# Eight wide products and then eight narrow ones, with the weight buffers 64 bytes apart, in a one-core hybrid trunk layer

## The chip, the cores and the metric

The kernel runs on one NeuronCore of a Trainium2 chip. The metric is the device time of one execution in microseconds (us). Engines are named as the profile names them: PE is TensorE's matmul, PEld its weight load, DVE is VectorE, ACT ScalarE, POOL GpSimd, SP SyncE, whose queue issues most DMAs.

## What is computed

One layer over 256 tokens of width 2048 in float32: a norm, a wide input projection whose columns feed four head groups, an output projection, a second norm and a SwiGLU.

```python
def reference(x, norm_mix_g, w_in, ..., w_out, norm_ffn_g, w_gate, w_up, w_down):
    h = x
    for l in range(DEPTH):                       # DEPTH = 1
        u = rmsnorm(h, norm_mix_g[l])
        h = h + hybrid_mixer(u, w_in[l], ..., w_out[l])   # conv, pooling, linear attention, attention
        u = rmsnorm(h, norm_ffn_g[l])
        h = h + swiglu_ffn(u, w_gate[l], w_up[l], w_down[l])
    return h

def swiglu_ffn(u, w_gate, w_up, w_down):
    return (jax.nn.silu(u @ w_gate) * (u @ w_up)) @ w_down
```

D_MODEL is 2048, D_FF 5632. The four groups are a gated convolution (A), multi-scale pooling (B), gated linear attention (C: its output is normed per head and gated) and forgetting attention (D).

## The kernel before

**Precision.** Every float32 value x that enters a large product is split into a rounded part hi (float32r, written by a cast on ACT) and the rest lo = x - hi (DVE). A product of weights and activations is then three products: weights hi with activations hi, weights hi with activations lo, weights lo with activations hi. Activations sit in SBUF as `u`, `y` and `hT`, shaped [128, k, 2, 256]: for each block k of 128 features first the 256 tokens' hi, then their lo. So hi weights are multiplied with 512 columns at once (hi and lo side by side, a *wide* product) and lo weights with 256 (a *narrow* product, added to the lo half of the same PSUM bank). `halves` adds the two halves of a bank at the end.

**Chunks.** All weights lie in one array `wall` of 376 chunks of 128 x 1024 in the order of use. `stage_through` issues for each the DMA into `raw` (4 buffers), the cast into `hi` on ACT (line 114) and the subtraction into `lo` on DVE (line 115), LOOK = 3 chunks ahead of use. `hi` and `lo` have four buffers each.

**Stages.** `block_lead` takes chunks 0 to 7, `block_tm` the next 40 (tokens on the partitions; its three products per k are all 512 columns wide, lines 203 to 205), then `block_fm` everything else: 8 blocks of the input projection (steps 2 or 4), 8 of the output projection with `y`, 44 of gate and up with `u`, and 8 of the down projection with `hT`. The last of these 8 is the `tail` (lines 169 to 171, all products 256 wide). A block of `block_fm` has 16 k (4 chunks) or 44 k (11 chunks), and for each k two column halves m, each into its own bank.

**The pair.** In `block_fm`, for each k and m a narrow product (`rest`, line 155) and a wide one (`whole`, line 152) follow each other; only at a block's first k the wide one goes first. There are 317 chunks of this kind with 8 pairs each: 2536 pairs.

```python
for f in (whole, rest) if first else (rest, whole):
    f()
```

**The work beside it.** Everything else of the mixer is written as generators in the queue `tasks` (`others` for pooling and convolution). After each chunk `side(n)` advances the first generator by n `yield`s, so a `yield` moves what follows it later in the stream of products. A recording layer then orders each engine's instructions by priority. Three pieces matter here:
- `gla_out` (group C): after the head norms (`rsqrt_of`, lines 226 to 237) it waits 4 yields, multiplies `sgg` and `ob` (lines 490 and 492), and after 5 more yields PE transposes `ob` (line 502).
- `token_rstd` (lines 239 to 254), run for both norms: PE sums squares (line 244), DVE and ACT form the reciprocal root, DVE writes two diagonal matrices `dg` (line 251), PE multiplies each with ones (line 252).
- `rsqrt_of` refines the root by one Newton step on DVE (four operations after the reciprocal).

**Addresses.** In the built program `u`, `y`, `hT` and all eight `hi` and `lo` buffers begin at byte 128 modulo 512 of a partition. The slice that a product reads as weights (128 columns, 512 bytes) or as moving columns begins a multiple of 512 bytes further on. So the two streams that PE reads beside each other begin at the same place modulo 512 in all of these products.

Of the kernel before, what the change touches and what calls it, by code (L numbers as in the profile page):

```python
# [9 lines left out]
F32 = mybir.dt.float32  # L10
BF16 = mybir.dt.bfloat16
F32R = mybir.dt.float32r
U8 = mybir.dt.uint8
AF = mybir.ActivationFunctionType
ALU = mybir.AluOpType
AX = mybir.AxisListType

P = 128
T = 256
# [39 lines left out]
def trunk_kernel(ctx: ExitStack, tc: tile.TileContext, a, out):  # L59
    nc = tc.nc  # L60
    V, S, PE = nc.vector, nc.scalar, nc.tensor
# [3 lines left out]
    ev = ctx.enter_context(tc.tile_pool(name="ev", bufs=2))  # L65
# [38 lines left out]
    def stage_through(n, ahead=AHEAD, parts=1):  # L104
        while issued[0] <= min(n, total - 1):
            i = issued[0]
            raw = wpool.tile([P, 1024], F32, name="raw", bufs=4)
            hi = wpool.tile([P, 1024], F32R, name="hi")
            lo = wpool.tile([P, 1024], F32R, name="lo")
            with tc.high_priority(offset=ahead):  # L110
                for q in range(parts):
                    c = slice(q * 1024 // parts, (q + 1) * 1024 // parts)
                    nc.sync.dma_start(out=raw[:, c], in_=a["wall"][i][:, c])
                    S.copy(out=hi[:, c], in_=raw[:, c])  # L114
                    V.tensor_tensor(out=lo[:, c], in0=raw[:, c], in1=hi[:, c].bitcast(F32), op=ALU.subtract)  # L115
            staged[i] = (hi, lo)
            issued[0] += 1
# [18 lines left out]
    def block_fm(rhs, order, steps=0, tail=False):  # L136
        b = [acc(), acc()]
        n = len(order)
        for c0 in range(0, n, 4):
            hi, lo = next_chunk()  # L140
            hi = hi.rearrange("p (k c) -> p k c", k=4)
            lo = lo.rearrange("p (k c) -> p k c", k=4)
            for kk in range(4):
                k = order[c0 + kk]
                first, last = c0 + kk == 0, c0 + kk == n - 1
                if tail:
                    continue
                for m in range(2):
                    cs = slice(m * P, (m + 1) * P)

                    def whole():
                        PE.matmul(b[m], lhsT=hi[:, kk, cs], rhs=rhs[:, k], start=first, stop=last)  # L152

                    def rest():
                        PE.matmul(b[m][:, T:], lhsT=lo[:, kk, cs], rhs=rhs[:, k, 0], start=False, stop=False,  # L155
                                  skip_group_check=True)

                    for f in (whole, rest) if first else (rest, whole):
                        f()
            if tail:  # L160

                turns = [(kk, m) for kk in range(4) for m in range(2)]
                if c0 + 4 == n:
                    turns = [(kk, m) for m in range(2) for kk in range(4)]
                for kk, m in turns:
                    k = order[c0 + kk]
                    cs = slice(m * P, (m + 1) * P)
                    o = b[m][:, :T]
                    PE.matmul(o, lhsT=hi[:, kk, cs], rhs=rhs[:, k, 0], start=c0 + kk == 0, stop=False)  # L169
                    PE.matmul(o, lhsT=hi[:, kk, cs], rhs=rhs[:, k, 1], start=False, stop=False)  # L170
                    PE.matmul(o, lhsT=lo[:, kk, cs], rhs=rhs[:, k, 0], start=False, stop=c0 + kk == n - 1)  # L171
            side(steps)
            side(1, others)
        return b
# [52 lines left out]
    def rsqrt_of(dst, src, pool, mul, n):  # L227

        w = pool.tile([P, 64 if pool is ev else 3 * n], F32, name=f"rs{n}")
        v, r, q = [w[:, i * n:(i + 1) * n] for i in range(3)]  # L230
        V.tensor_scalar(out=v, in0=src, scalar1=mul, scalar2=EPS, op0=ALU.mult, op1=ALU.add)
        S.activation(out=r, in_=v, func=AF.Sqrt)
        V.reciprocal(out=r, in_=r)
        V.tensor_tensor(out=q, in0=r, in1=r, op=ALU.mult)
        V.tensor_tensor(out=q, in0=q, in1=v, op=ALU.mult)
        V.tensor_scalar(out=q, in0=q, scalar1=-0.5, scalar2=1.5, op0=ALU.mult, op1=ALU.add)
        V.tensor_tensor(out=dst, in0=r, in1=q, op=ALU.mult)

    def token_rstd(sq):


        ps = misc()
        for t in range(2):
            PE.matmul(ps[:, t:t + 1], lhsT=sq[:, t * P:(t + 1) * P], rhs=con[:, C_ONE:C_ONE + 1], start=True, stop=True)
        rsqrt_of(rcol, ps[:, 0:2], ev, 1.0 / D, 2)
        yield
        yield
        ps2 = misc()
        for t in range(2):
            dg = ev.tile([P, P], F32, name="dg")  # L250
            V.tensor_scalar(out=dg, in0=ident, scalar1=rcol[:, t:t + 1], scalar2=None, op0=ALU.mult)
            PE.matmul(ps2[:, t * P:(t + 1) * P], lhsT=ones, rhs=dg, start=True, stop=True)
        S.copy(out=rb, in_=ps2[:, :T])
        yield
# [214 lines left out]
    def gla_out(gv, sgg):  # L469
# [14 lines left out]
            yield  # L484
        rs = mx.tile([P, 8], F32, name="grs")
        rsqrt_of(rs, ss, mx, 1.0 / P, 8)
        for _ in range(4):
            yield
        obv = ob.rearrange("p t h v -> p (t h) v")
        V.tensor_tensor(out=sgg, in0=sgg, in1=obv, op=ALU.mult)  # L490
# [339 lines left out]
```

## Time and profile before

| | |
|---|---|
| median of 3 runs | 1105.49 us (1104.51 to 1106.24) |
| the profiled execution | 1106.24 us, of which the span from first to last instruction is 1104.4 us |
| PE busy | 1096.7 us, 99% of the span |
| PEld, DVE, ACT busy | 86%, 65%, 48% |
| granted TensorE clock | 0.998 of full speed on the mean |
| DMA | 203.81 MB, 185 GB/s on the mean |

Matmuls overlap in the array and their recorded ends are modelled: a wide product is shown as 398 ns, though the next one starts some 230 ns later. So a busy PE says little, and what one product costs is read from the distance between the starts of two that follow each other. The 1.84 us between the time and the span lie before the first and behind the last instruction.

### The profile page before, as it was taken

The page shows a single profiled execution, that of the slowest core. Times are in us where ns is not written, and L with a number is a line of the kernel's source. Part 1 is how long each engine was busy: PE and PEld are TensorE (multiplying, and loading weights), DVE is VectorE, ACT ScalarE, POOL GpSimd, SP SyncE. Part 2 cuts the span into 40 slices and gives each one's busy share as a digit, 9 for nine tenths or more (in the row PEclk, how much of TensorE's full clock was granted, in tenths as well). Part 3 has the DMA queues.
Part 4 walks back from the last instruction along what each step waited for, and adds up shares of the span by engine and source line. Part 5 has one row for each costly group of instructions (what it writes and reads, how often), then busy time and mean ns, then how long its engine had stood idle before and what let it go on. Part 6 is the DMA issues. An engine that isn't in the chain of part 4 may idle for free.

```text
span 1104.4 us, 16172 instructions
## 1 busy us (share of the span) xinstructions
PE 1096.7 (99%) x6300; PEld 950.9 (86%) x6300; DVE 721.7 (65%) x1000; ACT 528.4 (48%) x726; POOL 36.3 (3%) x35
## 2 busy tenths in 40 slices
PE   9999999999999999999999999999999999999998
PEld 8887788888888888888888888888888888888898
DVE  8798867886777766666666666666666444555442
ACT  8545544454545544454445444454445343334441
POOL 0000000000443100000000000000000000000000
PEclk9999999999999999999999999999999999999999
DMA  8655355455565556655665565556556666666661
GB/s 310 213 177 161 126 172 172 159 166 175 187 191 188 176 190 191 186 184 185 189 191 183 185 187 189 190 181 185 188 191 185 184 195 200 199 200 198 199 190 62
DMA packets 59725, 203.81 MB, mean 185 GB/s; under 512 B 6768, under 2 KB 9216, under 8 KB 59648
## 3 DMA queue, kind: packets, MB, share of 16 engines
q1 hardware_dynamic: 59504, 202.75, 58.6%
q8 instruction: 49, 0.80, 0.3%
q14 instruction: 28, 0.23, 0.1%
q10 hardware_dynamic: 144, 0.03, 0.0%
HBM read 200.65 MB, written 2.10 MB: 184 GB/s over the span
## 4 chain that ended last, share of the span: by engine, by line
PE 97%; DVE 1%; DMA 1%; ACT 1%; issue 0%; SPq 0%; DVEq 0%; ACTq 0%
PE acc L152 54%; PE acc L155 27%; PE acc L203 3%; PE acc L204 3%; PE acc L205 3%; PE acc L186 1%; PE acc L171 1%; PE acc L169 1%; PE acc L170 1%; PE misc L401 1%; DMA raw<-in_wall 1%; DVE lo L115 0%; PE acc L662 0%; ACT hi L114 0%; PE misc L565 0%
## 5 line engine op out<-in xcount | busy, mean ns | idle before, releaser
L115 DVE TENSOR_TENSOR lo<-raw,hi 128x1024 fp32r<-128x1024 f32 (+1 forms) x384 | 463.6, 1209 | 311.6 <-ACT hi L114 303.6
L114 ACT CAST hi<-raw 128x1024 fp32r<-128x1024 f32 (+1 forms) x384 | 395.7, 1031 | 433.1 <-PE acc L152 254.5
L152 PE MATMUL acc<-u,hi 128*128 128x512 f32 x1664 | 583.6, 398 | 0.0
L155 PE MATMUL acc<-u,lo 128*128 128x256 f32 x1664 | 460.9, 282 | 0.0
L152 PEld LDWEIGHTS acc<-u,hi 128*128 128x128 f32 x1664 | 310.0, 188 | 70.4
L155 PEld LDWEIGHTS acc<-u,lo 128*128 128x128 f32 x1664 | 314.4, 189 | 4.8
L152 PE MATMUL acc<-hT,hi 128*128 128x512 f32 x616 | 215.5, 397 | 0.0
L155 PE MATMUL acc<-hT,lo 128*128 128x256 f32 x616 | 171.1, 280 | 0.0
L152 PEld LDWEIGHTS acc<-hT,hi 128*128 128x128 f32 x616 | 115.4, 188 | 27.2
L155 PEld LDWEIGHTS acc<-hT,lo 128*128 128x128 f32 x616 | 116.1, 189 | 0.6
L212 ACT COPY t<-acc 128x256 f32<-128x256 f32 x134 | 48.8, 364 | 96.1 <-PE acc L152 96.1
L152 PE MATMUL acc<-y,hi 128*128 128x512 f32 x256 | 89.9, 398 | 0.0
L214 DVE TENSOR_TENSOR t<-acc,t 128x256 f32<-128x256 f32 x134 | 56.3, 420 | 38.5 <-ACT t L212 38.5
L155 PE MATMUL acc<-y,lo 128*128 128x256 f32 x256 | 70.7, 281 | 0.0
L203 PE MATMUL acc<-hi,u 128*128 128x512 f32 x160 | 64.5, 403 | 0.0
L204 PE MATMUL acc<-hi,u 128*128 128x512 f32 x160 | 63.3, 395 | 0.0
L205 PE MATMUL acc<-lo,u 128*128 128x512 f32 x160 | 63.2, 395 | 0.0
L152 PEld LDWEIGHTS acc<-y,hi 128*128 128x128 f32 x256 | 47.7, 188 | 11.1
L155 PEld LDWEIGHTS acc<-y,lo 128*128 128x128 f32 x256 | 48.4, 189 | 0.7
L203 PEld LDWEIGHTS acc<-hi,u 128*128 128x128 f32 x160 | 30.3, 190 | 7.0
L205 PEld LDWEIGHTS acc<-lo,u 128*128 128x128 f32 x160 | 30.5, 191 | 6.5
L204 PEld LDWEIGHTS acc<-hi,u 128*128 128x128 f32 x160 | 30.4, 190 | 6.2 <-issue 0.3
(198 smaller groups left out, 625.9 us busy)
## 6 DMA issues: line engine op xcount, KB each, us to landing
raw<-in_wall SPq DMA_DIRECT2D x368, 512.0 KB, 3.5
raw<-in_wall SPq DMA_DIRECT2D x16, 256.0 KB, 5.4
out_T<-t SPq DMA_DIRECT2D x16, 128.0 KB, 2.6
xT<-in_xT SPq DMA_DIRECT2D x7, 256.0 KB, 5.4
con<-in_con SPq DMA_DIRECT2D x1, 480.0 KB, 5.7
msk_raw<-in_msk SPq DMA_DIRECT2D x1, 448.0 KB, 6.1
xT<-in_xT SPq DMA_DIRECT2D x2, 128.0 KB, 2.7
poolw<-in_poolw SPq DMA_DIRECT2D x1, 256.0 KB, 4.7
```

Of the source, the lines that this page charges most:

```text
L114: S.copy(out=hi[:, c], in_=raw[:, c])
L115: V.tensor_tensor(out=lo[:, c], in0=raw[:, c], in1=hi[:, c].bitcast(F32), op=ALU.subtract)
L152: PE.matmul(b[m], lhsT=hi[:, kk, cs], rhs=rhs[:, k], start=first, stop=last)
L155: PE.matmul(b[m][:, T:], lhsT=lo[:, kk, cs], rhs=rhs[:, k, 0], start=False, stop=False, skip_group_check=True)
L169: PE.matmul(o, lhsT=hi[:, kk, cs], rhs=rhs[:, k, 0], start=c0 + kk == 0, stop=False)
L170: PE.matmul(o, lhsT=hi[:, kk, cs], rhs=rhs[:, k, 1], start=False, stop=False)
L171: PE.matmul(o, lhsT=lo[:, kk, cs], rhs=rhs[:, k, 0], start=False, stop=c0 + kk == n - 1)
L203: PE.matmul(b[t], lhsT=u[:, k, 0, ts], rhs=hi[:, kk], start=k == 0, stop=False)
L204: PE.matmul(b[t], lhsT=u[:, k, 1, ts], rhs=hi[:, kk], start=False, stop=False)
L205: PE.matmul(b[t], lhsT=u[:, k, 0, ts], rhs=lo[:, kk], start=False, stop=k == KT - 1)
L212: S.copy(out=t1, in_=bank[:, T:])
L214: V.tensor_tensor(out=t2, in0=bank[:, :T], in1=t1, op=ALU.add)
```

## The change

Five edits, the first two the larger ones:
1. In `block_fm` (outside the tail) a chunk's 8 wide products are issued in a row, then its 8 narrow ones. In a block's last chunk the narrow ones go first, so that the wide ones can close the sum.
2. The eight weight buffers become eight tiles of their own, each 1040 elements long of which 1024 are used: each begins 4160 = 8 x 512 + 64 bytes behind the one before. In the built program `hi0, lo0, hi1, lo1, hi2, lo2, hi3, lo3` begin at 128, 192, 256, 320, 384, 448, 0 and 64 modulo 512. `u`, `y` and `hT` stay at 128.
3. The Newton step takes two DVE operations in place of three behind the square.
4. `dg` has one buffer in place of two (the space for edit 2), so the second waits until PE has read the first.
5. `gla_out` waits 8 yields in place of 4.

```diff
-            hi = wpool.tile([P, 1024], F32R, name="hi")
-            lo = wpool.tile([P, 1024], F32R, name="lo")
+            hi, lo = [wpool.tile([P, 1040], F32R, name=f"{v}{i % 4}", bufs=1)[:, :1024] for v in ("hi", "lo")]
...
-                    for f in (whole, rest) if first else (rest, whole):
-                        f()
+            if not tail:
+                turns = [(kk, m) for kk in range(4) for m in range(2)]
+
+                def whole():
+                    for kk, m in turns:
+                        PE.matmul(b[m], lhsT=hi[:, kk, m * P:(m + 1) * P], rhs=rhs[:, order[c0 + kk]],
+                                  start=c0 + kk == 0, stop=c0 + kk == n - 1)
+
+                def rest():
+                    for kk, m in turns:
+                        PE.matmul(b[m][:, T:], lhsT=lo[:, kk, m * P:(m + 1) * P], rhs=rhs[:, order[c0 + kk], 0],
+                                  start=False, stop=False, skip_group_check=True)
+
+                for f in (rest, whole) if c0 + 4 == n else (whole, rest):
+                    f()
...
-        V.tensor_tensor(out=q, in0=q, in1=v, op=ALU.mult)
-        V.tensor_scalar(out=q, in0=q, scalar1=-0.5, scalar2=1.5, op0=ALU.mult, op1=ALU.add)
-        V.tensor_tensor(out=dst, in0=r, in1=q, op=ALU.mult)
+        V.scalar_tensor_tensor(out=q, in0=q, scalar=-0.5, in1=v, op0=ALU.mult, op1=ALU.mult)
+        V.scalar_tensor_tensor(out=dst, in0=q, scalar=1.5, in1=r, op0=ALU.add, op1=ALU.mult)
...
-            dg = ev.tile([P, P], F32, name="dg")
+            dg = ev.tile([P, P], F32, name="dg", bufs=1)
...
-        for _ in range(4):
+        for _ in range(8):
             yield
```

PE's order at the second norm, near the start of gate and up, before: behind the sums of squares (line 244) eleven pairs of a narrow and a wide product follow, of which the last stand here, then both products with `dg`.

```order
L155 MATMUL acc<-u,lo 128x256
L152 MATMUL acc<-u,hi 128x512
L155 MATMUL acc<-u,lo 128x256
L152 MATMUL acc<-u,hi 128x512
L252 MATMUL misc<-dg,con 128x128 x2
L155 MATMUL acc<-u,lo 128x256
L152 MATMUL acc<-u,hi 128x512
```

The same place in the change (line numbers are one or two lower; `hi_3518` and so on are the buffers' uses):

```order
L243 MATMUL misc<-con,sq 128x1 x2
L150 MATMUL acc<-u,hi_3518 128x512 x8
L155 MATMUL acc<-u,lo_3519 128x256 x8
L150 MATMUL acc<-u,hi_3540 128x512
L251 MATMUL misc<-dg,con 128x128
L150 MATMUL acc<-u,hi_3540 128x512 x6
L251 MATMUL misc<-dg,con 128x128
L150 MATMUL acc<-u,hi_3540 128x512
L155 MATMUL acc<-u,lo_3541 128x256 x8
L155 MATMUL acc<-u,lo_3565 128x256 x8
L150 MATMUL acc<-u,hi_3564 128x512 x8
```

Wide and narrow products now come in runs of eight, two runs of narrow ones join where a block's last chunk begins, and the first product with `dg` stands behind 9 wide and 8 narrow products in place of 11 and 11, the second six wide ones later.

DVE's order at the same norm, before:

```order
L234 TENSOR_TENSOR rs_3591<-rs_3591 128x2
L235 TENSOR_TENSOR rs_3591<-rs_3591 128x2
L236 TENSOR_SCALAR rs_3591<-rs_3591 128x2
L237 TENSOR_TENSOR rcol<-rs_3591 128x2
L251 TENSOR_SCALAR dg<-con,rcol 128x128 x2
L115 TENSOR_TENSOR lo<-raw,hi 128x1024
```

And in the change:

```order
L234 TENSOR_TENSOR rs_3588<-rs_3588 128x2
L235 SCALAR_TENSOR_TENSOR rs_3588<-rs_3588 128x2
L236 SCALAR_TENSOR_TENSOR rcol<-rs_3588 128x2
L250 TENSOR_SCALAR dg<-con,rcol 128x128
L115 TENSOR_TENSOR lo_3641<-raw,hi_3640 128x1024
L250 TENSOR_SCALAR dg<-con,rcol 128x128
```

One short operation is gone, and the subtraction of a chunk stands between the two `dg`.

PE's order where `gla_out` transposes, in the stage of `block_tm`, with the buffers' numbers, before: the four transposes stand between the chunks `hi_1249` and `hi_1276` of the block that fills `acc_1136` and `acc_1137`.

```order
L203 MATMUL acc_1137<-hi_1249,u_71 128x512
L204 MATMUL acc_1137<-hi_1249,u_71 128x512
L205 MATMUL acc_1137<-lo_1250,u_71 128x512
L502 MATMUL misc_1331<-con_73,ob_1224 128x128 x2
L502 MATMUL misc_1336<-con_73,ob_1224 128x128 x2
L203 MATMUL acc_1136<-hi_1276,u_71 128x512
L204 MATMUL acc_1136<-hi_1276,u_71 128x512
```

In the change, where the block's last chunk is `hi3_1274`:

```order
L203 MATMUL acc_1136<-hi3_1274,u_71 128x512
L204 MATMUL acc_1136<-hi3_1274,u_71 128x512
L205 MATMUL acc_1136<-lo3_1275,u_71 128x512
L501 MATMUL misc_1347<-con_73,ob_1223 128x128 x2
L203 MATMUL acc_1355<-hi0_1292,u_71 128x512
L204 MATMUL acc_1355<-hi0_1292,u_71 128x512
```

The first transposes stand one chunk, 12 wide products, later: 58 such products lie between them and the products of line 481 in place of 46. On DVE the row of line 492 that they wait for now comes one short operation and one cast (line 384, which moved behind it) earlier.

## Rows read from the trace of the kernel before

**Rows 1.** The page: busy us, share of the span, instructions; granted clock by slices.
```profile
PE 1096.7 (99%) x6300; PEld 950.9 (86%) x6300; DVE 721.7 (65%) x1000; ACT 528.4 (48%) x726; POOL 36.3 (3%) x35
...
PEclk9999999999999999999999999999999999999999
```

**Rows 2.** The page: the chain that ended last, shares of the span by line.
```profile
PE acc L152 54%; PE acc L155 27%; PE acc L203 3%; PE acc L204 3%; PE acc L205 3%; PE acc L186 1%; PE acc L171 1%; PE acc L169 1%; PE acc L170 1%; PE misc L401 1%; DMA raw<-in_wall 1%; DVE lo L115 0%; PE acc L662 0%; ACT hi L114 0%; PE misc L565 0%
```

**Rows 3.** Timeline of PE, gate and up: start us, us, what; ten pairs.
```profile
499.62 0.40 PE L152 MATMUL acc<-u,hi 128*128 128x512 f32 x1
499.85 0.28 PE L155 MATMUL acc<-u,lo 128*128 128x256 f32 x1
499.97 0.40 PE L152 MATMUL acc<-u,hi 128*128 128x512 f32 x1
500.21 0.28 PE L155 MATMUL acc<-u,lo 128*128 128x256 f32 x1
...
503.15 0.40 PE L152 MATMUL acc<-u,hi 128*128 128x512 f32 x1
```

**Rows 4.** Timeline of PE in `block_tm`: first and 25th of a row of wide products.
```profile
127.30 0.39 PE L203 MATMUL acc<-hi,u 128*128 128x512 f32 x1
...
132.74 0.39 PE L203 MATMUL acc<-hi,u 128*128 128x512 f32 x1
```

**Rows 5.** Timeline of PE in the tail: first and 25th of a row of narrow products.
```profile
1080.28 0.28 PE L169 MATMUL acc<-hT,hi 128*128 128x256 f32 x1
...
1083.15 0.28 PE L169 MATMUL acc<-hT,hi 128*128 128x256 f32 x1
```

**Rows 6.** Line 152 by operand: ns min/median/max, first and last start us.
```profile
L152 PE MATMUL acc<-hT,hi x616: 387/395/404, 853.6 to 1069.2; 128*128 128x512 f32 x154
...
L152 PE MATMUL acc<-y,hi x256: 386/398/404, 266.2 to 356.2; 128*128 128x512 f32 x128
```

**Rows 7.** Timeline of PE in the down projection: first and 13th wide product of pairs.
```profile
1009.75 0.39 PE L152 MATMUL acc<-hT,hi 128*128 128x512 f32 x1
...
1013.91 0.39 PE L152 MATMUL acc<-hT,hi 128*128 128x512 f32 x1
```

**Rows 8.** Timeline of PE at a block's end: two wide products, then the next narrow one.
```profile
503.51 0.62 PE L152 MATMUL acc<-u,hi 128*128 128x512 f32 x2
...
503.97 0.28 PE L155 MATMUL acc<-u,lo 128*128 128x256 f32 x1
```

**Rows 9.** Timeline of PE at the transposes of `ob`; idle time and its releaser in brackets.
```profile
135.23 0.39 PE L205 MATMUL acc<-lo,u 128*128 128x512 f32 x1
137.58 0.63 PE L502 MATMUL misc<-con,ob 128*128 128x128 f32 x4 [1.96 <-DVE ob L492]
...
139.48 0.63 PE L205 MATMUL acc<-lo,u 128*128 128x512 f32 x1
...
142.04 0.51 PE L205 MATMUL acc<-lo,u 128*128 128x512 f32 x1
```

**Rows 10.** The stretch behind it: busy us of PE, PEld, DVE, ACT, POOL; granted clock; DMA.
```profile
138.90:142.20 3.30, 3.30 (x10) 2.52 (x9) 2.13 (x4) 0.69 (x1) 0.00 (x0) 0.50 0.59 174
```

**Rows 11.** Timeline of DVE ahead of those transposes.
```profile
135.90 0.28 DVE L384 CAST fhl<-fe 4x256 fp32r<-4x256 f32 x1
136.21 1.23 DVE L492 TENSOR_TENSOR ob<-sgg,grs 128x1024 f32<-128x1024 f32 x1
```

**Rows 12.** Timeline of DVE at the second norm.
```profile
374.13 0.16 DVE L237 TENSOR_TENSOR rcol<-rs 128x2 f32<-128x2 f32 x1
374.33 0.48 DVE L251 TENSOR_SCALAR dg<-con,rcol 128x128 f32<-128x128 f32 x2
```

**Rows 13.** Timeline of PE there: the first product behind the sums, and those with `dg`.
```profile
370.91 0.37 PE L155 MATMUL acc<-u,lo 128*128 128x256 f32 x1
...
374.81 0.61 PE L252 MATMUL misc<-dg,con 128*128 128x128 f32 x4
```

**Rows 14.** Who PE waited for: us in total, times, longest.
```profile
PE acc L186 <- ACT hi L114: 0.9, 2, 0.5
```

More of the change, by code (lines that the diff above doesn't have):

```diff
@@ L142, in block_fm @@
             lo = lo.rearrange("p (k c) -> p k c", k=4)
[L143 to L156, printed above, removed]
-                    for f in (whole, rest) if first else (rest, whole):
-                        f()
+            if not tail:
[10 more added lines that the diff above has]
+                    f()
             if tail:
```

## The prediction

> **What bounds the kernel now.** The page says it at once: PE is busy for 99% of the span, at the full granted clock in every slice [rows 1], and the chain that ended last lies for 54% in the wide products of line 152 and for 27% in the narrow ones of line 155 [rows 2]. A busy PE does not show what a product costs, so I read next the timeline of PE and take the distance from start to start. In gate and up ten pairs of a wide and a narrow product take 503.15 - 499.62 = 3.53 us, 353 ns a pair: some 235 for the wide one, 118 for the narrow one [rows 3]. Two other stages show what products of one width cost when they follow each other. In `block_tm` 24 wide ones take 132.74 - 127.30 = 5.44 us, 226.7 ns each [rows 4]; in the tail 24 narrow ones take 2.87 us, 119.6 ns each [rows 5]. Together 346.3, so 6.7 ns less than the pair in alternation. That difference, 2536 times, is what edit 1 is about.
>
> The alternation isn't always so slow: late in the down projection 12 pairs take 4.16 us, 346.7 ns each [rows 7]. The stage means say where that happens. Gate and up last from behind the last product with `y` (356.2 + 0.23) to the first with `hT` (853.6): 497.2 us for 1408 pairs, 353.1 each. The output projection takes 90.0 us for 255 distances, 352.9; the down projection 215.6 us for 615, 350.6 [rows 6]. The 256 pairs of the input projection I take at 353.1 too.
>
> Waits are few. In the list of who PE waited for, weights appear only at the start (0.9 us in the lead block) [rows 14]; the one large wait is 2.0 us for `ob` ahead of the transposes [rows 9]. Behind it the granted clock is 0.50 for 3.3 us [rows 10], the lower level, 1.2 GHz: there six wide products take 142.04 - 139.48 = 2.56 us, 427 ns each in place of 227 [rows 9].
>
> **Edit 1, the order.** 1664 pairs fall from 353.1 to 346.3 (-11.3 us), 256 from 352.9 (-1.7), 616 from 350.6 (-2.6): -15.6 us. Against it, a run's end still brings a change of width. A 4-chunk block keeps 6 changes and an 11-chunk block 20, together 60 x 6 + 7 x 20 = 500 in place of two per pair. If a change is what costs, it costs half of 6.8 ns, so 1.7 us are given back; if the cost lies elsewhere, nothing. At a block's end two wide products in a row, the first behind a narrow one, take 0.46 us, 7 ns above 2 x 226.7 [rows 8]; that is nearer to the upper bound, so I take +1.7. Net **-13.9 us**. Weights stay hidden: `hi` is released earlier in a chunk, `lo` at its end as before, and no stretch behind the lead block waits for either [rows 14]. Were that cover gone, each late chunk would stall PE by what is missing, and nothing in the trace comes near it.
>
> **Edit 2, the addresses.** All rows have both of PE's streams at the same place modulo 512, so none shows another. What can be read: at full clock a wide product costs 226.7 where 512 columns at 2.4 GHz are 213.3, 13.4 over; a narrow one 12.9 over. At half clock it costs 427, which is 512 columns at 1.2 GHz and nothing over [rows 4, 5, 9]. So something beside the columns costs 13 ns at full speed alone, for either width; the weight load that runs beside each product is a candidate, and whether the place modulo 512 matters to it is open. Bounds: the edit reaches 5072 + 480 + 192 + 264 = 6008 products, and 7 of 8 buffers leave the common place. If that removes all the excess, 6008 x 7/8 x 13.2 = 69 us are gained. If it costs, the worst wide product in these rows, 240 ns [rows 3], is 13.3 over the uniform one; on 7/8 of 3016 wide products that is +35 us. I take 0: the excess is equal at both widths and in three stages with other operands, which looks like a fixed price, and the trace has no row that speaks for either sign.
>
> The Trainium skill, page "TensorE: Matmul & The Clock Gate", section "Step-by-step: what each phase is for", says that PE reads weights and moving columns by two independent ports, and that loading the next weights takes no bandwidth from the running product. By that rule this edit would be worth nothing, the value taken above; the 13 ns over the columns at full clock show that something beside a product does cost, so the trace does not bear the rule out wholly.
>
> **Edits 3 and 5, the stall at `ob`.** PE reaches the transposes at 135.23 + 0.23 = 135.46 and starts them at 137.58, 2.0 us idle. In the change they stand 12 wide products later, so PE comes at 138.2. DVE ends line 492 at 136.21 + 1.23 = 137.44; one short operation (0.20, the step from one to the next in rows 12) and the cast (0.31) no longer stand ahead, so about 136.9 [rows 9, 11]. The wait goes, with 1.3 us to spare: **-2.0 us**. With it I expect the half clock to go, since nothing else of that size precedes it: 3.3 us hold 7.7 products that cost 0.2 too much: **-1.55 us**. Were the clock to fall anyway, only that last term would be lost. What is late next are the transposes themselves and `y` of group C, not needed before the output projection at 266 us.
>
> **Edits 3 and 4, the norms.** In the second one PE comes from the first product behind the sums (370.91) to `dg` after 9 wide and 8 narrow products, 9 x 0.2267 + 8 x 0.1196 = 3.0 us, at 373.91 instead of 374.81. DVE starts `dg` at 374.33, in the change 0.20 earlier, and needs half of 0.48 and a little: 374.4 [rows 12, 13]. PE waits **+0.5 us**, with gate and up queued behind. The second `dg` has 6 x 0.2267 = 1.4 us from PE's read to PE's need, in which DVE does a chunk's subtraction (1.23, as line 492 with the same size [rows 11]) and 0.25 of its own: between nothing and 0.5 us; I take nothing, since the chunk's buffers are released earlier than before. The first norm has the same form with one wide product less ahead, some +0.05.
>
> **Sum.** -13.9 - 2.0 - 1.55 + 0.5 + 0.05 = -16.9. The profiled execution took 1106.24 us, so 1089.3; it lies 0.75 above the median of the runs, and I say **1089 us**. Its own range is 1085 to 1093, from the 1.7 of the changes of width, 0.5 of `dg`, 1.55 of the clock and 1 us between runs. A difference of 0.2%, 2.2 us, is about what a measurement of this kernel can tell from no change.
>
> **Rivals.**
> - *The addresses give more.* For: the excess that vanishes at half clock, and a spacing that falls into one of two rhythms, 353 or 347, for the same pairs [rows 3, 7], as if the two streams' relative place mattered. Against: the equal excess at two widths. Time: 1089 less up to 69, 1020 to 1080. The same page, section "Back-to-back issue gap", gives a full-clock distance of columns / 2.4 + 2.5 ns for products alone; an estimate from it is 325 ns a pair, 54 us under the uniform 346.3 on the 2536 pairs. The rows show 346 at best.
> - *The order does nothing.* If the rhythm depends not on the widths but on how the runs happen to start, eights of one width may sit in the slow one as well; the down projection shows that alternation can run at 347 [rows 7]. Against: three stages of uniform width are all in the fast one. Then only stall and clock are won, 1106.2 - 3.0: 1103.
> - *The addresses cost*, and the kernel ends slower. Mechanism: with the weights starting behind the columns the two streams meet in mid product rather than side by side. Bound as above: 1089 + 35 = 1124. It decides from 17 us / (6008 x 7/8) = 3.2 ns a product on; half the distance between the two rhythms (3.2) is just that. For: the rhythms. Against: no row with another address shows it.
>
> **Chances.** Forecast 0.60, addresses give more 0.18, order does nothing 0.11, addresses cost 0.11. The range 1056 to 1104 holds the first, the third and a good half of the second. Faster by over 0.2%: 0.60 + 0.18 + half of 0.11, 0.84; within 0.2%: the other half and a little of the last, 0.07; slower 0.09.
>
> **What the changed profile would show.** Wide products 227 ns apart and narrow ones 120 in runs of eight, in all three stages; no wait of PE for `ob` and a granted clock of 1 throughout; half a microsecond ahead of `dg` at the second norm. If wide products stand under 220 ns apart, the addresses are what pays; if 230 or more, they or the runs cost. If distances differ between buffers 0 to 3, the place modulo 512 matters. A wait of PE for `hi` or `lo` would be something that I did not see.

## The result and the profile after

The changed kernel takes **1093.36 us** (median of 4 runs, 1092.44 to 1093.89), the kernel before 1105.87 beside it (4 runs, 1104.51 to 1106.54): ratio 0.9888, 95% interval 0.987 to 0.9905. The forecast was 1089.0 with 1056 to 1104. The profiled execution took 1092.44 us with a span of 1090.3, against 1106.24 and 1104.4, so 13.8 us less where the sum of the steps said 16.9. (In this section and below the changed kernel's lines are numbered as in its own code: wide products L150, narrow ones L155, the transposes of `ob` L501, the products with `dg` L251.)

The page of the changed kernel: busy time and share, then the granted clock in 40 slices, then the chain that ended last by line. They answer to [rows 1, 2]: PE is still the bound, at full clock, with the same shares of wide and narrow products.

```profile
PE 1084.9 (100%) x6300; PEld 944.3 (87%) x6300; DVE 707.6 (65%) x996; ACT 519.8 (48%) x726; POOL 31.1 (3%) x35
...
PEclk9999999999999999999999999999999999999999
...
PE acc L150 54%; PE acc L155 27%; PE acc L203 3%; PE acc L205 3%; PE acc L204 3%; PE acc L171 1%; PE acc L170 1%; PE acc L169 1%; PE misc L400 1%; ACT hi L114 1%; DMA raw<-in_wall 1%; ACT u L267 0%; DVE lo L115 0%; PE acc L661 0%; PE misc L564 0%
```

The changed kernel's wide products by operand (ns min/median/max, first and last start in us), as [rows 6]. Gate and up now last from 352.7 + 0.23 to 842.7, 489.8 us where they took 497.2; the down projection 213.3 instead of 215.6.

```profile
L150 PE MATMUL acc<-hT,hi x616: 387/392/404, 842.7 to 1056.0; 128*128 128x512 f32 x154
L150 PE MATMUL acc<-y,hi x256: 387/392/404, 264.1 to 352.7; 128*128 128x512 f32 x128
```

The timeline of its PE over one block of gate and up (start us, us, what), as [rows 3]. A row is a run; what one product costs is the distance to the next row's start, divided by the count.

```profile
501.19 2.02 PE L150 MATMUL acc<-u,hi 128*128 128x512 f32 x8
503.05 1.07 PE L155 MATMUL acc<-u,lo 128*128 128x256 f32 x8
503.95 2.00 PE L150 MATMUL acc<-u,hi 128*128 128x512 f32 x8
505.80 2.04 PE L155 MATMUL acc<-u,lo 128*128 128x256 f32 x16
507.68 3.84 PE L150 MATMUL acc<-u,hi 128*128 128x512 f32 x16
511.36 1.11 PE L155 MATMUL acc<-u,lo 128*128 128x256 f32 x8
512.30 2.02 PE L150 MATMUL acc<-u,hi 128*128 128x512 f32 x8
```

32 pairs take 11.11 us, 347.2 ns each, where alternation had 353. But the runs differ by buffer, which is in no term of the sum: the narrow run at 503.05 (`lo1`) stands at some 113 ns, the one at 511.36 (`lo0`) at 117.5; the wide one at 501.19 (`hi1`) at 232.5, the sixteen at 507.68 (`hi3`, then `hi0`) at 230. Only the last seven of these sixteen, whose weights begin at the columns' place, come to the 226.7 of [rows 4]: 511.36 - 509.77 = 1.59 us, 227 each.

```profile
509.77 1.75 PE L150 MATMUL acc<-u,hi 128*128 128x512 f32 x7
```

Over all of gate and up the distance behind a wide product was 235.3 ns on the mean before and is 230.5 now, behind a narrow one 117.3 and 116.8.

`block_tm`, whose order did not change, became slower by place alone: 24 wide products of the changed kernel take 132.57 - 127.03 = 5.54 us, 230.8 ns each, against 226.7 in [rows 4]; over the stage the mean distance is 231.3 against 227.8. In the tail 24 narrow ones take 1067.85 - 1065.01 = 2.84 us, 118.3 each, against 119.6 in [rows 5]; over the tail it is 116.9 against 120.0.

```profile
127.03 0.40 PE L203 MATMUL acc<-hi,u 128*128 128x512 f32 x1
...
132.57 0.39 PE L203 MATMUL acc<-hi,u 128*128 128x512 f32 x1
...
1065.01 0.28 PE L169 MATMUL acc<-hT,hi 128*128 128x256 f32 x1
...
1067.85 0.27 PE L169 MATMUL acc<-hT,hi 128*128 128x256 f32 x1
```

At the transposes of `ob`, the timeline of PE and then the window that [rows 10] show for before: PE no longer waits there, the clock stays at 1.00, and 0.19 us of a wait for `y`, behind the later transposes, are what is left of [rows 9].

```profile
138.58 0.40 PE L205 MATMUL acc<-lo,u 128*128 128x512 f32 x1
138.82 0.38 PE L501 MATMUL misc<-con,ob 128*128 128x128 f32 x2
...
144.97 0.44 PE L501 MATMUL misc<-con,ob 128*128 128x128 f32 x2 [0.19 <-DVE y L224]
```

```profile
138.90:142.20 3.30, 3.30 (x19) 2.67 (x18) 3.27 (x5) 3.30 (x7) 0.00 (x0) 1.00 0.59 201
```

At the second norm, PE and then DVE of the changed kernel, as [rows 12, 13]: `dg` was written by 369.53 + 0.28 = 369.81, and PE came for it at 370.33 without a wait. At the first norm PE waits 0.38 us for `dg` (the last row below; 0.17 before).

```profile
367.21 2.11 PE L150 MATMUL acc<-u,hi 128*128 128x512 f32 x8
...
370.33 0.38 PE L251 MATMUL misc<-dg,con 128*128 128x128 f32 x2
```

```profile
369.53 0.28 DVE L250 TENSOR_SCALAR dg<-con,rcol 128x128 f32<-128x128 f32 x1
```

```profile
37.29 0.46 PE L251 MATMUL misc<-dg,con 128*128 128x128 f32 x2 [0.38 <-DVE dg L250]
```

### The profile page after: what moved, and what is told of

It reads as the page before. It is cut to its first block, busy times and chain, and to the rows that moved or that the text cites. A ratio compares the mean times of both kernels' runs of the same rounds, so it can differ in the third digit from the quotient of the medians.

```text
span 1090.3 us, 16159 instructions
## 1 busy us (share of the span) xinstructions
PE 1084.9 (100%) x6300; PEld 944.3 (87%) x6300; DVE 707.6 (65%) x996; ACT 519.8 (48%) x726; POOL 31.1 (3%) x35
## 4 chain that ended last, share of the span: by engine, by line
PE 96%; ACT 2%; DVE 1%; DMA 1%; issue 0%; SPq 0%; DVEq 0%; ACTq 0%
PE acc L150 54%; PE acc L155 27%; PE acc L203 3%; PE acc L205 3%; PE acc L204 3%; PE acc L171 1%; PE acc L170 1%; PE acc L169 1%; PE misc L400 1%; ACT hi L114 1%; DMA raw<-in_wall 1%; ACT u L267 0%; DVE lo L115 0%; PE acc L661 0%; PE misc L564 0%
## 5 line engine op out<-in xcount | busy, mean ns | idle before, releaser
L150 PE MATMUL acc<-u,hi 128*128 128x512 f32 x1664 | 412.5, 394 | 0.0
L150 PEld LDWEIGHTS acc<-u,hi 128*128 128x128 f32 x1664 | 301.5, 188 | 58.1
L155 PEld LDWEIGHTS acc<-u,lo 128*128 128x128 f32 x1664 | 217.1, 188 | 12.6
L155 PE MATMUL acc<-u,lo 128*128 128x256 f32 x1664 | 221.2, 280 | 0.0
L150 PE MATMUL acc<-hT,hi 128*128 128x512 f32 x616 | 153.7, 393 | 0.0
L150 PEld LDWEIGHTS acc<-hT,hi 128*128 128x128 f32 x616 | 110.7, 188 | 20.8
L155 PEld LDWEIGHTS acc<-hT,lo 128*128 128x128 f32 x616 | 81.5, 188 | 5.7
L155 PE MATMUL acc<-hT,lo 128*128 128x256 f32 x616 | 82.7, 279 | 0.0
L150 PE MATMUL acc<-y,hi 128*128 128x512 f32 x256 | 63.0, 392 | 0.0
L150 PEld LDWEIGHTS acc<-y,hi 128*128 128x128 f32 x256 | 46.4, 188 | 9.0
L155 PEld LDWEIGHTS acc<-y,lo 128*128 128x128 f32 x256 | 33.3, 188 | 1.9
L155 PE MATMUL acc<-y,lo 128*128 128x256 f32 x256 | 33.8, 279 | 0.0
```

What stands on the lines that cost most here:

```text
L150: PE.matmul(b[m], lhsT=hi[:, kk, m * P:(m + 1) * P], rhs=rhs[:, order[c0 + kk]], start=c0 + kk == 0, stop=c0 + kk == n - 1)
L155: PE.matmul(b[m][:, T:], lhsT=lo[:, kk, m * P:(m + 1) * P], rhs=rhs[:, order[c0 + kk], 0], start=False, stop=False, skip_group_check=True)
```

## The experiments

The places are given as hi/lo, in bytes behind the activations modulo 512; "eights" is the order of edit 1, "pairs" the old one. The ns column is the gate-and-up stage, from its first product to the first with `hT`, divided by its 1408 pairs; it holds a little other work, the same in all kernels. Ratios are to the runs of before made beside each kernel; their medians were 1106.11 us (e1 to e3), 1106.02 (e5 to e7, e9), 1105.59 (e10 to e12) and 1106.49 (e13).

| run | order | places | edits 3, 5 | ns a pair | time, us | ratio to before, 95% |
|---|---|---|---|---|---|---|
| before | pairs | 0/0 | no | 353.1 | 1105.87 | |
| e1_order | eights | 0/0 | no | 349.2 | 1099.38 | 0.9944, 0.9928 to 0.9961 |
| e5_parity | sixteens | 0/0 | no | 348.6 | 1096.05 | 0.9913, 0.9898 to 0.9928 |
| e6_fours | fours | 0/0 | no | 351.0 | 1103.22 | 0.9973, 0.9964 to 0.9983 |
| e11_everything_64 | eights | 0/0, all moved | no | 349.3 | 1098.27 | 0.9933, 0.9921 to 0.9946 |
| e9_all_weights_64 | eights | 64/64 | no | 347.5 | 1092.30 | 0.9882, 0.9865 to 0.9898 |
| e2_addresses | pairs | eight places | no | 349.6 | 1098.87 | 0.9936, 0.9921 to 0.995 |
| e10_alternating_64 | pairs | 64/64 | no | 353.7 | 1109.33 | 1.0035, 1.0021 to 1.0049 |
| e13_alternating_lo64 | pairs | 0/64 | no | 348.1 | 1095.80 | 0.9903, 0.9888 to 0.9919 |
| e3_side | pairs | 0/0 | yes | 353.3 | 1104.88 | 0.9991, 0.9982 to 1.0001 |
| e7_lo192 | eights | 0/192 | yes | 348.9 | 1096.02 | 0.9911, 0.9896 to 0.9926 |
| e12_64_and_side | eights | 64/64 | yes | 347.4 | 1090.88 | 0.9869, 0.9855 to 0.9882 |
| the change | eights | eight places | yes | 347.9 | 1093.36 | 0.9888, 0.987 to 0.9905 |

**The parts of the change alone.** After the result two theories stood: A, that order alone gives the uniform spacing and the addresses cost on top; B, that the addresses do nothing and the runs of eight themselves cost. e1_order is the kernel before with edit 1.

> The kernel before with the order alone (eight wide products, then eight narrow ones); addresses, Newton step, dg and the yields stay as before. Theory A (the changed addresses cost the wide products about 4 ns and save the narrow ones about 3): with all streams at one place modulo 512 wide products stand 227 ns apart and narrow ones 120, a pair 347; 2536 pairs gain 14 us, the stall at ob and the half clock stay: 1092 us. Theory B (addresses do nothing, a run of eight costs what the change shows, 348 to 349 a pair): 12.5 less the 3.5 of the stall is gained, 1097 us, and wide products stand 231 apart, narrow ones 117.

e2_addresses is the kernel before with edit 2 and one buffer for `dg` (edit 4).

> The kernel before with the new addresses of the eight weight buffers alone (and one dg buffer for the space); the order stays wide and narrow in turn. Theory A: the distances change with the buffer, wide products of block_tm stand 231 to 232 apart in place of 227 (+2 us), narrow ones of the tail 117 (-0.7 us), and the pairs move by some ns either way: 1100 to 1112 us. Theory B: nothing moves, 1106 us, and all four buffers read alike.

e3_side is the kernel before with edits 3 and 5 (the shorter Newton step and the 8 yields).

> The kernel before with the shorter Newton step and 8 yields in place of 4 in gla_out; order and addresses as before. If the stall and the half clock behind it are what they seem, both go: 2.0 + 1.55 us less, 1102.3 us, granted clock 1.0. If DVE is late for something else instead, a wait of about 2 us stands at another place and the time is within 1 us of before.

Order alone won 6.7 us, addresses alone 7.2, the side work 1.2; 15.1 added up, while all at once win 12.5. Neither theory holds whole: A is wrong in that order alone falls 7 us short and addresses alone win (its 231 ns in `block_tm` and 117 in the tail came), B in that addresses do a lot. What order alone lacks is seen in the timeline of e1_order's PE. The first row is a run of eight wide products behind narrow ones; the second shows its last three, the third the narrow run behind it, and the last one the wide run with which the next 32 pairs begin, as the run at 502.91 did.

```profile
502.91 2.00 PE L150 MATMUL acc<-u,hi 128*128 128x512 f32 x8
...
505.71 2.00 PE L150 MATMUL acc<-u,hi 128*128 128x512 f32 x8
...
506.87 0.84 PE L150 MATMUL acc<-u,hi 128*128 128x512 f32 x3
...
507.55 2.08 PE L155 MATMUL acc<-u,lo 128*128 128x256 f32 x16
...
514.07 2.00 PE L150 MATMUL acc<-u,hi 128*128 128x512 f32 x8
```

The first five take 506.87 - 505.71 = 1.16 us, 232 ns each; the last three 0.68, 226.7 each. Over the trace's runs of eight behind narrow ones in the products with `u`, some hundred, the mean distances are 233, 236, 228, 232, 231 and then 227, 227, 227: five products settle, and cost 27 ns together. A narrow run begins 113 to 117, 119 and then stays at 120. So 32 pairs take 514.07 - 502.91 = 11.16 us, 348.8 each, not 346.3.

e4_map_a is the whole change with other places, hi at 0, 32, 64, 96 and lo at 128, 160, 192, 224, the tiles taken ahead.

```diff
+            if i == 0:
+                sizes = [1032, 1032, 1032, 1032, 1032, 1032, 1032, 1096]
+                for n, v in enumerate([f"{v}{j}" for v in ("hi", "lo") for j in range(4)]):
+                    width[v] = sizes[n]
+                    ready[v] = wpool.tile([P, sizes[n]], F32R, name=v, bufs=1)
```

> The changed kernel with the buffers hi0 to hi3 at 0, 32, 64 and 96 bytes behind the place of the activations modulo 256, lo0 to lo3 at 128, 160, 192 and 224. In the change's own trace hi0 (0) stands at 227 to 230, hi1 (128) at 232, lo1 (192) at 114, lo0 (64) at 117.5, and buffers 256 apart read alike. Theory A: each buffer has its own distance again, lo2 (192) 114, hi0 (0) 227; the others are new, wide between 216 and 240, narrow between 109 and 121. Theory B: all four wide ones alike at 231 and all four narrow ones alike at 117.

One execution, 1113.91 us: it has two waits of 2.7 and 4.6 us in `block_lead` (35.7 us long instead of 24.5), so its time says nothing of the places. Gate and up took 495.2 us against the change's 489.8: these places are worse there. Theory A's own numbers did not come: in gate and up `lo2`, at 192, stands at 118 ns on the mean and not at 114, and `hi0`, at 0, at 232 and not at 227. The means of the four wide buffers lie within 2 ns, and so do those of the four narrow ones, near Theory B's 231 and 117.

**Do the changes of width cost (theory C) or only alternation (D)?** Two doses, both with edit 1 on the old addresses. e5_parity:

```diff
-                for f in (rest, whole) if c0 + 4 == n else (whole, rest):
+                for f in (rest, whole) if c0 + 4 == n or c0 // 4 % 2 else (whole, rest):
```

> Edit 1 alone on the old addresses, but every second chunk begins with its narrow run, so that two runs of a width join: 162 changes from narrow to wide where edit 1 has 250. Theory C (each change from narrow to wide costs about 28 ns, spread over the next five wide products, and the change back gives 7): 88 x 21 ns less than edit 1 alone, 1097.5 us, with the first five of each wide run again some 6 ns each over 227. Theory D (only that the widths no longer alternate matters, not how many changes are left): 1099.4 us as edit 1 alone.

e6_fours loops over halves of a chunk:

```diff
-                turns = [(kk, m) for kk in range(4) for m in range(2)]
+                for half in range(2):
+                    turns = [(2 * half + kk, m) for kk in range(2) for m in range(2)]
...
-                for f in (rest, whole) if c0 + 4 == n else (whole, rest):
+                    for f in (rest, whole) if c0 + 4 == n and half else (whole, rest):
```

> Edit 1 alone on the old addresses, but in runs of four instead of eight: 567 changes from narrow to wide. Theory C: each costs about 23 ns over four wide products less 7, so 567 x 16 = 9.1 us over uniform spacing, where runs of eight have 250 x 21 = 5.2; 1103 us (1102 to 1104.5), wide products at 233, 236, 228, 233 and none at 227. Theory D: 1099.4 us as runs of eight.

1096.05 and 1103.22: the time follows the number of changes, as C says. In the profiled stages with such pairs the sixteens win 1.7 us over the eights where 1.85 were expected, and the fours lose 4.5 (3.9). The fours' wide products stand at 234, 234, 232 and 228, none at 227, not quite the four distances that C named. The medians of e5 and e1 lie 3.3 apart, but three of e1's four executions had a stretch below full clock (below), none of e5's.

**Which place counts?** e9 moves the eight weight buffers together, e11 everything; both are e1 with one buffer for `dg` and a pad, first e9's, then e11's.

```diff
             raw = wpool.tile([P, 1024], F32, name="raw", bufs=4)
+            if i == 0:
+                wpool.tile([P, 16], F32, name="pad0", bufs=1)
             hi = wpool.tile([P, 1024], F32R, name="hi")
             lo = wpool.tile([P, 1024], F32R, name="lo")
+            if i == 0:
+                wpool.tile([P, 112], F32, name="pad2", bufs=1)
```

```diff
+    keep.tile([P, 16], F32, name="pad0")
     xT = keep.tile([P, KT, T], F32, name="xT")
```

> Edit 1 alone, with one buffer for dg, and all eight weight buffers moved together by 64 bytes, activations where they were. Theory C (the distance from the columns counts): narrow runs at 117.5 ns in every buffer instead of 120, 6 us less; wide runs somewhere between the 227 of distance 0 and the 233 of distance 128, so nothing to 15 us more; 1093 to 1109 us. Theory E (only the places of the weight buffers among each other count): every distance as with edit 1 alone, narrow 120, wide settling to 227, and 1099.4 us.

> Edit 1 alone, with one buffer for dg, and all buffers moved by 64 bytes, activations and weights together, so that the distance between them stays 0. Theory C (the distance between weights and columns counts): as edit 1 alone, 1099.4 us, narrow 120 ns and wide ones settling to 227. Theory H (the place itself counts): as with the weights alone at 64, 1092.3 us, narrow 113 and wide 231 and 236 in turn.

e9 ran at 1092.30, e11 at 1098.27 with e1's distances to the nanosecond (233, 236, 228, 232, 231, 227 and narrow 120). So it is the distance between weights and columns that counts, not the place; in e9 the weights also moved against the other buffers that stayed, such as `raw`, and no run parts the two. Theory C was right in kind but not in size: narrow runs were expected at 117.5 and came at 113.4. The tail shows the place by itself, since all its products are narrow: 24 take 2.72 us in e9, 113.3 each, and 2.88 in e11, 120.0 each. That is 1.7 of the 6.0 us between the two runs. Rows of e9's tail (line 173), then of e11's (line 170):

```profile
1059.82 0.28 PE L173 MATMUL acc<-hT,hi 128*128 128x256 f32 x1
...
1062.54 0.28 PE L173 MATMUL acc<-hT,hi 128*128 128x256 f32 x1
...
1065.00 0.28 PE L170 MATMUL acc<-hT,hi 128*128 128x256 f32 x1
...
1067.88 0.28 PE L170 MATMUL acc<-hT,hi 128*128 128x256 f32 x1
```

The timeline of e9's PE (its wide products are L154, its narrow ones L159):

```profile
502.09 2.02 PE L154 MATMUL acc<-u,hi 128*128 128x512 f32 x8
503.95 1.07 PE L159 MATMUL acc<-u,lo 128*128 128x256 f32 x8
...
506.73 1.98 PE L159 MATMUL acc<-u,lo 128*128 128x256 f32 x16
508.55 3.89 PE L154 MATMUL acc<-u,hi 128*128 128x512 f32 x16
...
513.19 2.02 PE L154 MATMUL acc<-u,hi 128*128 128x512 f32 x8
```

Sixteen narrow ones take 1.82 us, 113.8 each, and eight wide ones 1.86, 232.5 each: the narrow ones are shorter by about what the wide ones are longer. The wide ones stand at 231 and 236 in turn without end, begin at 226, and do not settle. 32 pairs take 11.10 us, 346.9: what the place won over e1 in the pairs is the settling, since a wide and a narrow product in steady runs add up to 346.7 in both.

e7_lo192 is the whole change with hi at 0 and lo at 192, where the changed kernel's shortest narrow run had stood.

```diff
             hi = wpool.tile([P, 1024], F32R, name="hi")
+            if i == 0:
+                wpool.tile([P, 48], F32, name="pad1", bufs=1)
             lo = wpool.tile([P, 1024], F32R, name="lo")
+            if i == 0:
+                wpool.tile([P, 80], F32, name="pad2", bufs=1)
```

> All five edits, but with other addresses: the four hi at the activations' place modulo 512 and the four lo 192 bytes behind it. Theory C (a narrow product's spacing depends on how far its weights lie from its columns modulo 256: 113.5 ns at 192, 120 at 0; a wide one's is best at 0): narrow runs at 113.5 ns in all buffers and stages, wide ones settling to 227 as with edit 1 alone, 1082 to 1086 us. Theory D (the short spacing in one buffer came from the neighbours that it had in that layout, not from its distance): narrow runs at 117 to 120 and 1092 to 1099 us.

1096.02: Theory C in this form fell. The narrow runs stood at 118 ns on the mean, not 113.5, though their weights lay 192 behind the columns as in the changed kernel's lo1. There the wide run ahead, hi1 at 128, stands at 229 and 237 in turn; here hi at 0 stands between 225 and 234 in a run of eight and comes near 227 only late in a run of sixteen. A product's distance to the next is thus no function of its own place alone; what else sets it, the run ahead or the weights of the other kind, no run shows. The changed kernel says the same: `lo3`, at 448, stands at 114 with `hT`, mostly behind a wide run, and at 117.7 in gate and up, where it always follows `lo2` at 117.8.

**Does alternation cost at all?** e10 is the old order with e9's places, e13 the old order with hi at 0 and lo at 64 (as the diff of e7, with pads of 16 and 112 elements).

> The old order, a narrow and a wide product in turn, with all eight weight buffers 64 bytes behind the activations' place and one buffer for dg. Theory F (what costs at a change of width is the settling at distance 0; at 64 the first wide product after narrow ones stands at 226 ns and the first narrow one after wide ones at 118): 344 ns a pair instead of 352.4, 2536 x 8.4 = 21 us less than before, 1085 us. Theory G (alternation costs at any distance): 348 to 352 a pair as with the mixed addresses of edit 2 alone, 1096 to 1106 us.

> The old order, a narrow and a wide product in turn, with the four hi at the activations' place, the four lo 64 bytes behind it, and one buffer for dg. Edit 2 alone ran at 348.4 ns a pair, with all weights at 0 or all at 64 it is 352.4 and 353.5. Theory I (in alternation it counts that the weights of two products in a row stand at different places): as edit 2 alone, 348 ns a pair, 1096 to 1099 us. Theory J (only the distance of each product's weights from its columns counts, and what edit 2 alone won lies in the buffers at other distances): 118 + 235 = 353 ns a pair, 1104 to 1108 us.

e10 is 0.35% slower than before, against Theory F; e13 wins 10.7 us by four moved buffers (the four lo) alone, as Theory I says. Timelines of PE, e10's and then e13's:

```profile
499.95 0.40 PE L156 MATMUL acc<-u,hi 128*128 128x512 f32 x1
...
503.49 0.40 PE L156 MATMUL acc<-u,hi 128*128 128x512 f32 x1
```

```profile
500.02 0.39 PE L156 MATMUL acc<-u,hi 128*128 128x512 f32 x1
...
502.79 0.39 PE L156 MATMUL acc<-u,hi 128*128 128x512 f32 x1
```

Ten pairs in 3.54 us are 354 each (235 and 118 or 119), eight in 2.77 are 346.3 (228 to 231 and 116 to 118). In gate and up alternation is slow where both kinds of weights stand at one place, whichever, and as quick as uniform runs where they stand 64 bytes apart.

With both at the columns' place it is not slow everywhere. In the down projection of before, the second, fourth and sixth of the seven blocks in pairs run at 346.7 ns a pair from their second chunk on ([rows 7] lie in the sixth), the other four at 353. In the seventh 12 pairs take 1048.04 - 1043.80 = 4.24 us, 353.3 each:

```profile
1043.80 0.40 PE L152 MATMUL acc<-hT,hi 128*128 128x512 f32 x1
...
1048.04 0.40 PE L152 MATMUL acc<-hT,hi 128*128 128x512 f32 x1
```

In e3_side, with the same order and places, the same three blocks are quick; in e10 none is, in e13 all seven are. So at 0/0 the same products keep one of two rhythms through a whole block, and what picks it stays open.

**Stall and clock.** The trace of e3_side shows the stall at `ob` gone and full clock there, in this window (columns as in [rows 10]):

```profile
133.00:150.00 17.00, 16.70 (x77) 13.28 (x76) 16.11 (x30) 9.64 (x15) 0.00 (x0) 1.00 0.61 185
```

But that execution had two other waits, 1.7 us at the start and 1.3 at line 361; the list of who PE waited for, and the second wait in before (line 362 there):

```profile
PE acc L186 <- ACT hi L114: 2.1, 2, 1.7
PE misc L361 <- issue: 1.3, 1, 1.3
...
PE misc L362 <- issue: 0.4, 1, 0.4
```

In before these were 0.9 [rows 14] and 0.4, so in this one execution as much was lost elsewhere as the stall had cost. The half clock of [rows 10] is not there in every execution: of the 44 runs of before that stood beside the experiments 24 had a mean clock below 1.000, with a median of 1106.6 us, and 20 had 1.000, with 1105.0. Of the 22 executions of kernels with edit 5 (e3, e7, e12 and the change) one had less than 1.000: the profiled one of e3, where the stretch came at 11 us, behind the wait of 1.7 at the start. Where the stretch lies is known from traces alone: of the nine with a wait of 1.7 to 2.0 us at the transposes, three (before, e10, e11) have 3.4 us at 0.50 behind it, and six have none there; e13 has such a stretch at 12 us, behind a wait of 1.85 at the start.

**Best of both.** e12_64_and_side is the whole change with e9's pads in place of the eight tiles.

> All five edits, with all eight weight buffers 64 bytes behind the activations' place instead of at eight places. From the same without edits 3 and 5 (1092.3 us) less the 1.2 us that these were worth alone, up to the 3.5 of stall and half clock: 1089 to 1091 us under Theory C, narrow runs at 113 ns and wide ones at 231 and 236 in all stages. If eight different places are better than one for a reason that these distances do not show, 1093 us or more.

1090.88 us (1090.64 to 1091.06), 14.7 below before and 2.5 below the change by the medians. The two ratios' intervals overlap by a little, so that it beats the change is likely rather than settled; in the traces gate and up is 0.6 us shorter and the tail 0.9.

## Why the prediction was right, and where its terms were wrong

**Edit 1, the order: right in kind, mis-sized.** "If a change is what costs, it costs half of 6.8 ns, so 1.7 us are given back" is the step that failed. A change from narrow to wide costs some 27 ns over five products and the one back gives about 7, so 250 x 20 = 5.0 us are given back at the old addresses; e5 and e6 show the dose. [Rows 8] show two products behind a change and could not show five. A second fault: the input projection was taken at 353.1 a pair without a row. Before, its products stood at some 231 and 117 on the mean, 348 a pair (other work stands between them, which may be why); that stage won nothing (+0.3 us) where -1.6 was in the sum. A third is small: the steady narrow product stands at 120.0, which the rounded starts of [rows 5] show as 119.6, so a uniform pair costs 346.7 and not 346.3. Order alone gave -7.3 us in the four stages, not -13.9; of the 6.6 us between them the three faults are 3.3, 1.9 and 0.9. The rival "the order does nothing" falls with e1_order's 6.7 us; its ground, that the same pairs keep one of two rhythms, holds in the blocks of the down projection above.

**Edit 2, the addresses: the value taken, 0, was wrong.** Alone they win 7.2 us. With both edits the four stages win 7.4 + 2.35 + 1.45 - 0.3 = 10.9 us, 3.6 more than order alone. In gate and up it is the narrow products that gain, 116.8 ns on the mean against e1_order's 119.3, while the wide ones lose, 230.5 against 229.3. The settling isn't gone: `hi2`, 256 behind, stands at 233, 236, 228, 233, 230 and then 227 in the run at 503.95. The addresses cost 480 x 3.5 ns = 1.7 us in `block_tm` and give 0.8 in the tail. So 3.6 - 1.7 + 0.8 = 2.7 of the 6.6 us that edit 1 fell short were made up by an edit that was priced at nothing: that the total came near is in this part luck. The result lies in the stated range and just above the 1085 to 1093 that the forecast called its own. The rival "the addresses give more" had named the right sign ("as if the two streams' relative place mattered"), but its time, under 1080, was not reached, and neither did wide products fall under 220 ns. "The addresses cost" came true for wide products alone, by 3.5 ns in `block_tm` and by 1.2 in gate and up beside e1_order. Of the signs named, distances that differ between buffers came, and so did wide products at 230 or more.

The Trainium skill, page "TensorE: Matmul & The Clock Gate", section "Step-by-step: what each phase is for", has weights and moving columns on two independent ports, by which the place would be worth nothing. e11 against e9 does not agree: the same order and the same buffers, with the weights' distance from the columns changed from 0 to 64 bytes, 1098.3 and 1092.3 us; whether it is at the ports that the place counts, no run shows. The Trainium skill, same page, section "Back-to-back issue gap", gives columns / 2.4 + 2.5 ns for a product alone, by which an estimate is 215.8 and 109.2. No steady run came nearer than 226.7 and 113.3, and none of these had both at once.

**Edits 3 and 5: the wait right, the price little more than a third.** The stall went as foreseen, and the transposes and `y` became what is late next (0.19 us). The clock term was right in size, 1.6 us between the runs of before with and without it, but it belongs to about half of the executions. e3 shows 1.2 us (the ratio's interval allows -0.1 to 2.0), e12 against e9 1.4, where 3.55 was said; in the two profiled executions of before and the change it came whole, since `block_tm` is 1.9 us shorter although the addresses cost 1.7 there. In the traces the stall is gone; the waits at the start and at line 361 differ from one trace to the next by 1 to 2 us, and that this is what hides the rest was seen in one execution and isn't shown for the median.

**Edits 3 and 4, `dg`: wrong by 0.5.** No wait at the second norm. Before, DVE began `dg` 374.33 - 370.91 = 3.42 us behind PE's first product after the sums; the step took that over, less 0.20. After, it is 369.53 - 367.21 = 2.32, since in the middle of that chain DVE's subtraction of a chunk no longer waits 0.58 us for its cast, nor the reciprocal 0.29 for ACT. At the first norm, where +0.05 was said, the wait for `dg` grew by 0.2 us, from 0.17 to 0.38; in the other traces with one buffer for `dg` it lies between 0 and 0.8.

**Sum by stages**, profile to profile: gate and up -7.4 (said, with `dg`, -8.2), down -2.35 (-2.1), output -1.45 (-1.5), input +0.3 (-1.6), `block_tm` -1.9 (-3.5), tail -0.8 (0), lead -0.4 (0): -14.0 in place of -16.9.

## What to carry to other kernels

Read the cost of a product from distances of starts, buffer by buffer and by position in a run, since a mean over a row of the timeline hides a settling of five products and a spread between buffers. Where weights of two kinds alternate, try their buffers 64 bytes apart modulo 512 before reordering anything: here that alone won 10.7 us, more than the new order alone. The gains of two edits that cure the same thing don't add: in gate and up order alone brings the pair from 353 to 349 ns, places alone to 348 (e13), and both together to 347.4 at best (e12).

## What the runs showed of the hardware

- At full clock the distance of two float32r products goes with where their weights stand relative to the moving columns: in steady runs a narrow one took 120.0 ns at distance 0 (e11's tail) and 113.3 at 64 (e9's), a wide one 226.7 at 0 and 231 and 236 in turn at 64. The sum of a pair is 346 to 347 in three arrangements (runs at 0 once settled, runs at 64, alternation at 0/64). In alternation at one place it is 353 to 354, but 346.7 in three of seven blocks of before's down projection.
- Places 256 bytes apart read alike with `hT` in the changed kernel: lo at 64 and 320 both 117.6, hi at 128 and 384 both 229 and 237 in turn. In gate and up, where runs of two chunks join, lo at 192 and 448 do not (113.4 and 117.7), so the place alone doesn't fix the distance.
- After narrow products, wide ones with weights at distance 0 (e1_order, e11) need five products to settle.
- A run keeps a rhythm of two steps (231 and 236 at distance 64) over sixteen products, and alternation at 0/0 keeps one of two rhythms, 347 or 353 a pair, through a block of 88 pairs. What in the array, the ports or the memory makes it stays open; no run here separates a wide product's own weights from those being loaded beside it.
- A wait of about 2 us ahead of the transposes was followed by a stretch of 3.4 us at 1.2 GHz in three of nine traces, not in all. Of the executions of before 24 of 44 had a mean clock below 1.000; for those without a trace the place of the stretch isn't known.
